# Which token blocks are gathered, and which engine sums the second expert table, in a one-layer decoder step

## The chip, the cores and the metric

The kernel runs on one core of one Trainium2 chip. The metric is the device time of one execution in microseconds; three runs of the kernel before gave 4419.91, 4423.67 and 4437.72, median 4423.67. The profile is of one more execution, of 4433.77 us.

## What is computed

One inference step of a decoder trunk with one layer, on 1024 prompt tokens (blocks 0 to 7 of 128) and 64 sample tokens (8 sequences of 8, "the sample block", numbered 8), with the same weights, D = 1024, all float32.

```
n = rmsnorm(x);  z = n @ w_in
h = x + w_out( sum over 3 branches of sigmoid(gate_b) * P_b(branch_b(n)) )
    branches: gated linear attention (GLA, with a running state),
              forgetting softmax attention (FoX, prompt: causal over earlier blocks;
                                            sample: over a paged cache of 1024 tokens),
              attention over 256 memory tokens
xn = rmsnorm(h)
per token, 8 heads: top 16 of 16384 experts by two sets of 128 keys -> eidx, softmax weights g
a = gelu(xn . u_tab[eidx]);  h += sum over the 128 chosen of (g*a) * v_tab[eidx]
y = rmsnorm(h)
```

Outputs are y, and the new caches and states of prompt and sample.

## The kernel before, in words

**Token groups.** The layer runs over three groups of blocks, `GROUPS = [[0,1,2], [3,4,5], [8,6,7]]` (line 42), one call of `base` (line 636) each, so that a weight tile, loaded once per group, serves up to 384 tokens. `mm_w` (line 256) loads 512 KB of weights (line 262), splits them into a high and a low part on ScalarE and VectorE (lines 265, 267), and TensorE multiplies three products of high and low parts in fp32r (lines 273 to 285). The branches of a block are float32: `gla` (389), `fox_prompt` (550, work grows with the block's number), `mem_prompt_att` (595). The sample block has its own: `gla_sample` (484, its state products at lines 493 and 507), `fox_sample` (1240) and `mem_sample` (1363), which fetch cache pages through GpSimd's queue (line 1237) and sum values in partition strips of one PSUM bank (lines 1348, 1403). `base` ends with h and the normed rows stored (`h_scr`, `x2_scr`), and the key scores, reduced to the best 16 on the way by `top16` (902).

**Experts, two ways.** Gathered blocks (0, 1, 2 beside the layer, 6 and 7 beside the dense pass) are done by `peer_gather` (1028): for each of the 128 choices of a token, GpSimd fetches one row of the first table for all 128 tokens (an indirect DMA of 512 KB, line 1040), VectorE multiplies it with the token's row and sums (1042), ScalarE takes the gelu (1044); then GpSimd fetches the row of the second table (1051) and VectorE adds it, scaled, to `acc` (1057). Four row buffers are used in turn (five in the dense pass). Dense blocks (`DENSE = [3, 4, 5, 8]`, 448 tokens) go through `peer_dense` (1122), which streams both tables through TensorE (lines 1166 to 1216) and multiplies by a weight matrix of tokens and experts. That matrix is made by `expert_weights` (1071) in rounds of 16 tokens: one-hot tiles on VectorE and ScalarE, 16 float32 matmuls (1117) into the PSUM bank `cw`, copies (1118), one store to `c_scr` (1120). For a dense block of the last group (`HERE`, the sample) this is done within `peer_dense`, before its main loop.

**The order.** Each engine's order of instructions is laid down ahead by a planner that plays the program through in time with costs of its own and takes, of the ready instructions, the one with the lowest priority number. `at` (1420) sets that number: the layer has the lowest, `choose` and `expert_weights` follow, gathers come last, block by block (`gather`, 1431):

```
    for grp in GROUPS:
        base(grp)
        ...
        if mine and grp is not GROUPS[-1]:
            gather(mine)
    early.close()
    with ExitStack() as ctx2:
        ...
        peer_dense(ctx2, dn)
```

`early.close()` gives the layer's eight PSUM banks and its work tiles to the dense pass. SP issues all other transfers, in one queue; GpSimd's queue has the indirect ones.

## Time and profile before

| What | Value |
|---|---|
| median of 3 runs | 4423.67 us |
| profiled execution | 4433.77 us |
| its span, first to last instruction | 4432.0 us |
| TensorE busy in the span | 3755.6 us (85%) |
| VectorE busy | 3346.1 us (75%) |
| ScalarE, GpSimd busy | 1796.2 us (41%), 1679.1 us (38%) |
| granted TensorE clock, mean | 0.890 |
| DMA, mean over the span | 258 GB/s |

PE is TensorE's matmul, PEld its weight load, DVE VectorE, ACT ScalarE, POOL GpSimd, SP the engine that issues transfers. Busy time is the union of an engine's instructions; matmul ends are modelled. The granted clock is the share of full speed (2.4 GHz) that TensorE was given; its other level is 1.2 GHz. A float32 matmul appears as two records, an fp32r one as one. Times within the span are counted from its first instruction: group 0 of the layer lies at 0 to 704 us, group 1 at 704 to 1695, group 2 at 1695 to 2960, and then comes the dense pass.

### The profile page before, as it was taken

The numbers are of one execution on the slowest core, as the hardware profiler recorded it, in microseconds if no ns is written. First come the engines' busy times: TensorE is split into PE (matmuls) and PEld (weight loads), VectorE is DVE, ScalarE is ACT, GpSimd is POOL, SyncE is SP. The second block draws the span as 40 slices with busy tenths as digits, with TensorE's granted clock in tenths as the row PEclk, the third lists the DMA queues.
The fourth block names the chain that finished last, engine by engine and source line by source line (L and its number), as shares of the span: only waits on it lengthen the run. The fifth ranks groups of instructions, "written<-read, shape, count | busy, mean of one in ns | idle before, by whom it ended". The sixth has DMA issues, their size and how long they took to land. (4 is left out here: it accounts for less than half of the span.)

```text
span 4432.0 us, 62344 instructions
## 1 busy us (share of the span) xinstructions
PE 3755.6 (85%) x21306; PEld 3288.8 (74%) x21306; DVE 3346.1 (75%) x7924; ACT 1796.2 (41%) x3637; POOL 1679.1 (38%) x1466
## 2 busy tenths in 40 slices
PE   4998998676689775787679979986999999999998
PEld 4886997564378775575556558875999899999997
DVE  3443469988788898888885457578999888888883
ACT  2555444343343333465564334444333223323332
POOL 0000003545644444534455553003445454545530
PEclk8997998787689886677689989997999999999999
DMA  3322457888899987778788899548999999999982
GB/s 110 90 84 70 131 165 227 279 274 294 277 309 332 319 267 242 260 243 273 253 277 287 307 321 320 169 140 289 329 303 339 327 332 337 341 337 327 344 297 81
DMA packets 652340, 1141.32 MB, mean 258 GB/s; under 512 B 62158, under 2 KB 445798, under 8 KB 648439
## 3 DMA queue, kind: packets, MB, share of 16 engines
q0 software_dynamic: 193616, 704.99, 45.6%
q1 hardware_dynamic: 458406, 432.35, 30.3%
q8 instruction: 169, 2.77, 0.2%
q14 instruction: 149, 1.21, 0.1%
HBM read 1073.45 MB, written 63.74 MB: 257 GB/s over the span
## 5 line engine op out<-in xcount | busy, mean ns | idle before, releaser
L1040 POOL DMA_INDIRECT u<-in_peer_u_dram,ei x640 | 783.3, 1224 | 873.2 <-DVE a L1042 347.6
L1051 POOL DMA_INDIRECT v<-in_peer_v_dram,ei x640 | 762.3, 1191 | 865.0 <-DVE acc L1057 452.6
L1042 DVE CUSTOM_DVE_ANT_0 u<-u,x 128x1024 f32<-128x1024 f32 x640 | 774.2, 1219 | 129.9 <-DMA u<-in_peer_u_dram,ei 128.3
L1057 DVE SCALAR_TENSOR_TENSOR acc<-v,a,acc 128x1024 f32<-128x1024 f32 x635 | 811.6, 1278 | 70.6 <-DMA v<-in_peer_v_dram,ei 68.2
L265 ACT ACTIVATE wh<-wr 128x512 fp32r<-128x512 f32 x568 | 354.0, 630 | 595.0 <-PE pj L274 186.2
L267 DVE TENSOR_TENSOR wl<-wr,wh 128x512 fp32r<-128x512 f32 x568 | 386.6, 685 | 219.4 <-PE pj L277 63.8
L1210 PE MATMUL py<-dwh,dvh 128*128 128x448 f32 x1024 | 373.9, 370 | 31.3 <-ACT dwh L1197 28.6
L1187 PE MATMUL pa<-xh,duh 128*128 128x448 f32 x1024 | 384.8, 376 | 1.3 <-ACT duh L1168 1.3
L1188 PE MATMUL pa<-xl,duh 128*128 128x448 f32 x1024 | 379.0, 370 | 0.0
L273 PE MATMUL pj<-aT,wh 128*128 128x384 f32 (+1 forms) x1104 | 367.3, 337 | 11.4 <-ACT X L837 4.5
L1211 PE MATMUL py<-dwl,dvh 128*128 128x448 f32 x1024 | 375.4, 367 | 1.4 <-DVE dwl L1198 1.4
L1212 PE MATMUL py<-dwh,dvl 128*128 128x448 f32 x1024 | 373.4, 368 | 0.3 <-DVE dvl L1206 0.3
L274 PE MATMUL pj<-aT,wh 128*128 128x384 f32 (+1 forms) x1104 | 362.3, 332 | 1.7 <-DVE aT L317 1.7
L281 PE MATMUL pj<-wh,aT 128*128 128x256 f32 x944 | 262.1, 301 | 30.3 <-DVE z L720 10.9
L1205 ACT ACTIVATE dvh<-dvr 128x1024 fp32r<-128x1024 f32 x128 | 134.2, 1059 | 377.2 <-PE py L1211 206.6
L282 PE MATMUL pj<-wh,aT 128*128 128x256 f32 x944 | 258.8, 297 | 2.9 <-DVE aT L847 1.5
L277 PE MATMUL pj<-aT,wl 128*128 128x384 f32 (+1 forms) x1104 | 251.8, 335 | 10.3 <-DVE wl L267 10.1
L1117 PE MATMUL cw<-hot,hot 128*128 128x128 f32 x768 | 173.9, 363 | 92.7 <-ACT stg L1118 73.8
L1190 PE MATMUL pa<-xh,dul 128*128 128x448 f32 x1024 | 240.2, 369 | 0.0
L1117 PEld LDWEIGHTS cw<-hot,hot 128*128 128x128 f32 x768 | 134.8, 248 | 138.1 <-ACT stg L1118 103.3
L1210 PEld LDWEIGHTS py<-dwh,dvh 128*128 128x128 f32 x1024 | 192.4, 189 | 48.6 <-ACT dwh L1197 28.9
L273 PEld LDWEIGHTS pj<-aT,wh 128*128 128x128 f32 x1104 | 213.1, 193 | 17.4 <-ACT X L837 6.6
(475 smaller groups left out, 8439.3 us busy)
## 6 DMA issues: line engine op xcount, KB each, us to landing
wr<-in_w_in_dram SPq DMA_DIRECT2D x168, 512.0 KB, 4.8
dvr<-in_peer_v_dram SPq DMA_DIRECT2D x128, 512.0 KB, 7.5
dur<-in_peer_u_dram SPq DMA_DIRECT2D x128, 512.0 KB, 6.6
dc<-c_scr SPq DMA_DIRECT2D x15, 1792.0 KB, 17.4
wr<-in_w_pq_dram SPq DMA_DIRECT2D x48, 512.0 KB, 4.3
c_scr<-stg SPq DMA_DIRECT2D x24, 1024.0 KB, 6.9
wr<-in_w_out_dram SPq DMA_DIRECT2D x24, 512.0 KB, 4.8
u<-in_peer_u_dram,ei POOLq DMA_INDIRECT x640, 6.2
```

Source lines behind the costliest of these rows:

```text
L267: V.tensor_tensor(wl, raw[:, q2:q2 + 2], wh.bitcast(F32), op=OP.subtract)
L273: PE.matmul(ps, wh[:, i, c], hi[:, k], start=k == 0, stop=False)
L274: PE.matmul(ps, wh[:, i, c], lo[:, k], start=False, stop=False)
L1040: G.indirect_dma_start(out=r, out_offset=None, in_=UR, in_offset=bass.IndirectOffsetOnAxis(ap=ei[:, s:s + 1], axis=0))
L1042: V.tensor_tensor_reduce(r, r, x2, 1.0, 0.0, OP.mult, OP.add, a[:, s:s + 1])
L1051: G.indirect_dma_start(out=r, out_offset=None, in_=VR, in_offset=bass.IndirectOffsetOnAxis(ap=ei[:, s:s + 1], axis=0))
L1057: V.scalar_tensor_tensor(acc, r, a[:, s:s + 1], acc, op0=OP.mult, op1=OP.add)
L1187: PE.matmul(pa[:, :NT], uh[:, k], xh[:, k], start=k == 0, stop=False)
L1188: PE.matmul(pa[:, :NT], uh[:, k], xl[:, k], start=False, stop=False)
L1210: PE.matmul(py[:, :NT], vh[:, j], wh, start=j == 0, stop=False)
L1211: PE.matmul(py[:, :NT], vh[:, j], wl, start=False, stop=False)
L1212: PE.matmul(py[:, :NT], vl[:, j], wh, start=False, stop=j == DG - 1)
```

## The change

The sample block goes into the first group, `GROUPS = [[8,0,1], [2,3,4], [5,6,7]]`. Gathered beside the layer are still 0, 1 and 2 (0 and 1 after group 0, 2 after group 1); beside the dense pass 5 and 6 instead of 6 and 7, by `peer_gather` as before. Dense are 8, 3, 4 and 7; block 7 takes the sample's part as the dense block of the last group.

For 0, 1 and 2, `choose` writes indices and weights in another layout: 64 tokens at a time, partitions 0 to 63 with a token's first four heads and 64 to 127 with its last four. `gather_u` is as before but by halves of a block (64 fetches of 128 rows each). `gather_v` fetches 64 times as well, and TensorE sums: the stationary is a 128x64 matrix with a token's two scales in its column (`st`, eight at a time on VectorE), the moving operand is the fetched row, its first 512 columns going to partitions 0 to 63 of the bank `cw` and its last 512 to 64 to 127. `turns` takes one fetch of the second table's half and one of the next half's first table by turns. `expert_weights` in the layer uses the banks `g` instead of `cw`; the sample's choice and expert weights get the last priority of all; the ring `tp` has two buffers instead of three; `acc` of `peer_gather` lies in the dense pass's pool.

```diff
--- before.py
+++ after.py
@@ -39,13 +39,13 @@
 
 ROWS, ROWS2 = 4, 5
 SAMPLE = 8
-GROUPS = [[0, 1, 2], [3, 4, 5], [SAMPLE, 6, 7]]
-
-DENSE = [3, 4, 5, SAMPLE]
-
-LATER = [6, 7]
-
-HERE = [SAMPLE]
+GROUPS = [[SAMPLE, 0, 1], [2, 3, 4], [5, 6, 7]]
+
+DENSE = [SAMPLE, 3, 4, 7]
+
+LATER = [5, 6]
+
+HERE = [7]
 DG, DW = 8, 9
 WR = 4
 CB = {"hot": 4, "stg": 1, "eg": 1}
@@ -70,8 +70,8 @@
     pp = early.enter_context(tc.tile_pool(name="pp", bufs=8, space=bass.MemoryType.PSUM))
     bp = early.enter_context(tc.tile_pool(name="bp", bufs=1))
 
-    BUFS = {"aT": 2, "wr": WR, "wh": 4, "wl": 2, "z": 4, "zq": 1, "zt": 4, "tq": 2, "tp": 3, "oT": 3, "kv": 2, "pg": 2,
-            "la": 2, "ge": 3, "lh": 4, "kE": 2, "gq": 1, "att": 2, "X": 2, "XL": 2, "P": 4, "PT": 3, "sm": 12,
+    BUFS = {"aT": 2, "wr": WR, "wh": 4, "wl": 2, "z": 4, "zq": 1, "zt": 4, "tq": 2, "tp": 2, "oT": 3, "kv": 2, "pg": 2,
+            "la": 2, "st": 2, "ah": 2, "ge": 3, "lh": 4, "kE": 2, "gq": 1, "att": 2, "X": 2, "XL": 2, "P": 4, "PT": 3, "sm": 12,
             "sm2": 1, "sm5": 1}
     PSB = {"pj": 2, "g": 2, "f": 2, "po": 1, "cw": 1}
     cnt = [0]
@@ -975,7 +975,7 @@
                     V.match_replace(k[:, hd], s[:, hd, 0:8], k[:, hd], 0.0)
                     V.max(s[:, hd, 8:16], k[:, hd])
             c = slice(hf * 64, (hf + 1) * 64)
-            if b in DENSE:
+            if b in DENSE or b not in LATER:
                 ei, gw = w[:, 528:592].bitcast(I32), region(656, 16)
             else:
                 ei, gw = eidx[b][:, c], gate_w[b][:, hs]
@@ -994,19 +994,26 @@
             if b in DENSE:
                 SP.dma_start(e_scr[b][:, c], ei)
                 SP.dma_start(g_scr[b][:, c], w[:, 656:720])
+            elif b not in LATER:
+
+                for i in range(2):
+                    o, x = slice(64 * hf, 64 * hf + 64), slice(64 * i, 64 * i + 64)
+                    V.tensor_copy(eidx[b][o, 64 * i:64 * i + 64], ei[x])
+                    V.tensor_copy(gate_w[b][o, 4 * i:4 * i + 4], gw[x])
 
 
     UR, VR = peer_u[0], peer_v[0]
 
     turn = [0]
     lanes = [gp] * ROWS
+    dense_pool = []
 
     def big(name):
 
         cnt[0] += 1
         turn[0] += 1
         if name in ("x2", "acc"):
-            return gp.tile([128, 1024], F32, tag=name, name=f"{name}_{cnt[0]}", bufs=1)
+            return (gp if name == "x2" else dense_pool[0]).tile([128, 1024], F32, tag=name, name=f"{name}_{cnt[0]}", bufs=1)
         i = turn[0] % len(lanes)
         return lanes[i].tile([128, 1024], F32, tag=f"row{i}", name=f"{name}_{cnt[0]}", bufs=1)
 
@@ -1068,6 +1075,67 @@
         SP.dma_start(gfin, rows(g_final, 1024))
         finish(b, acc, ht, gfin)
 
+
+    halves_of = [(0, 64), (64, 128)]
+
+    def gather_u(b, half, a):
+
+        x2 = big("x2")
+        for lo, hi in halves_of:
+            SP.dma_start(x2[lo:hi], x2_scr[b][64 * half:64 * half + 64])
+        ei, gw = eidx[b], gate_w[b]
+        for hd in range(4):
+            for k in range(16):
+                s = hd * 16 + k
+                r = big("u")
+                G.indirect_dma_start(out=r, out_offset=None, in_=UR,
+                                     in_offset=bass.IndirectOffsetOnAxis(ap=ei[:, 64 * half + s:64 * half + s + 1], axis=0))
+                V.tensor_tensor_reduce(r, r, x2, 1.0, 0.0, OP.mult, OP.add, a[:, s:s + 1])
+                if k == 15:
+                    sl = slice(hd * 16, (hd + 1) * 16)
+                    A.activation(a[:, sl], a[:, sl], AF.Gelu_apprx_tanh)
+                    V.tensor_tensor(a[:, sl], a[:, sl], gw[:, 4 * half + hd, :], op=OP.mult)
+                yield
+
+    def gather_v(b, half, a):
+
+
+        ei = eidx[b]
+        acc = PS("cw")
+
+        PE.matmul(acc, nd[64:65, :128].bitcast(F32), iof[64:65, None, :].to_broadcast([1, 4, 128]), start=True, stop=False)
+        for s in range(64):
+            if s % 8 == 0:
+                st = T("st", [128, 8, 64])
+                V.tensor_tensor(st, id2[:, None, :].to_broadcast([128, 8, 64]),
+                                a[:, s:s + 8, None].to_broadcast([128, 8, 64]), op=OP.mult)
+            r = big("v")
+            G.indirect_dma_start(out=r, out_offset=None, in_=VR,
+                                 in_offset=bass.IndirectOffsetOnAxis(ap=ei[:, 64 * half + s:64 * half + s + 1], axis=0))
+            for i, (lo, hi) in enumerate(halves_of):
+                PE.matmul(acc[lo:hi], st[:, s % 8], r[:, 512 * i:512 * i + 512], start=False, stop=s == 63)
+            yield
+
+        t = big("h")
+        ht, gfin = t[:, :512], t[:, 512:]
+        rs = slice(64 * half, 64 * half + 64)
+        for i, (lo, hi) in enumerate(halves_of):
+            SP.dma_start(ht[lo:hi], h_scr[b][rs, 512 * i:512 * i + 512])
+            SP.dma_start(gfin[lo:hi], bass.AP(tensor=g_final.tensor, offset=g_final.offset + 512 * i,
+                                              ap=[[0, 64], [1, 512]]))
+        V.tensor_tensor(ht, acc, ht, op=OP.add)
+        s1 = gp.tile([128, 2], F32, tag="fs", name=f"fs{b}_{half}", bufs=2)
+        s2 = gp.tile([128, 2], F32, tag="fr", name=f"fr{b}_{half}", bufs=2)
+        A.activation(acc, ht, AF.Square, accum_out=s1[:, 0:1])
+        for i, (lo, hi) in enumerate(halves_of):
+            V.tensor_copy(s2[lo:hi, 0:1], s1[64 - lo:128 - lo, 0:1])
+        V.tensor_tensor(s1[:, 1:2], s1[:, 0:1], s2[:, 0:1], op=OP.add)
+        G.tensor_scalar(s2[:, 1:2], s1[:, 1:2], 1.0 / D, EPS, op0=OP.mult, op1=OP.add)
+        G.tensor_tensor(s2[:, 1:2], s2[:, 1:2], neghalf[:, :1], op=OP.pow)
+        V.scalar_tensor_tensor(ht, ht, s2[:, 1:2], gfin, op0=OP.mult, op1=OP.mult)
+        for i, (lo, hi) in enumerate(halves_of):
+            SP.dma_start(y_prompt[0, b * 128 + 64 * half:b * 128 + 64 * half + 64, 512 * i:512 * i + 512], ht[lo:hi])
+
     def expert_weights(b, H=None, psum=None):
 
         w = 64 if b == SAMPLE else 128
@@ -1078,7 +1146,7 @@
             return bp.tile(shape, dt, tag=tag, name=f"{tag}_{cnt[0]}", bufs=CB[tag])
 
         H = H or H_base
-        psum = psum or (lambda: PS("cw"))
+        psum = psum or (lambda: PS("g"))
 
 
         q, e, f = H("hot", [128, 2, 128]), H("hot", [128, 2, 128]), H("hot", [128, 2, 128])
@@ -1413,6 +1481,8 @@
 
     iof = const([128, 128], F32, cp)
     G.iota(iof, pattern=[[1, 128]], base=0, channel_multiplier=0, allow_small_or_imprecise_dtypes=True)
+    id2 = const([128, 64], F32, cp)
+    V.tensor_tensor(id2, ident[:, :64], ident[:, 64:], op=OP.add)
     mem_kv()
     M = 10 ** 6
     urgent = [M // 2]
@@ -1427,6 +1497,7 @@
 
 
     prio = [M]
+    rest = [100 * M]
 
     def gather(blocks):
         for i, b in enumerate(blocks):
@@ -1435,6 +1506,26 @@
                 at(prio[0] + M // 2, choose, blocks[i + 1])
             at(prio[0], peer_gather, b)
         prio[0] += M
+
+    def gather_halves(blocks):
+
+        v = iter(())
+        for i, b in enumerate(blocks):
+            for half in range(2):
+                prio[0] += M
+                if half and i + 1 < len(blocks):
+                    at(prio[0] + M // 2, choose, blocks[i + 1])
+                a = T("ah", [128, 64])
+                at(prio[0], turns, gather_u(b, half, a), v)
+                v = gather_v(b, half, a)
+        prio[0] += M
+        at(prio[0], turns, v)
+        prio[0] += M
+
+    def turns(*its):
+        its = list(its)
+        while its:
+            its = [x for x in its if next(x, its) is not its]
 
     for grp in GROUPS:
         pj3[0] = grp is GROUPS[0]
@@ -1448,16 +1539,23 @@
         for b in first:
             if b in DENSE and grp is GROUPS[-1]:
                 choose(b)
-            else:
-                at(None, choose, b)
-            if b in DENSE and grp is not GROUPS[-1]:
-                at(None, expert_weights, b)
+                continue
+
+            late = b == SAMPLE
+            if late:
+                rest[0] += M
+            at(rest[0] if late else None, choose, b)
+            if b in DENSE:
+                if late:
+                    rest[0] += M
+                at(rest[0] if late else None, expert_weights, b)
         if mine and grp is not GROUPS[-1]:
-            gather(mine)
+            gather_halves(mine)
     early.close()
     with ExitStack() as ctx2:
         dn = ctx2.enter_context(tc.tile_pool(name="dn", bufs=1))
         lanes += [dn] * (ROWS2 - ROWS)
+        dense_pool.append(dn)
         if mine:
             gather(mine)
         peer_dense(ctx2, dn)
```

## Rows read from the trace of the kernel before

**Rows 1.** Busy us by stage: PE, PEld, DVE, ACT, POOL, (counts); clock, DMA share, GB/s.

```profile
704.00:1695.00 991.00, 747.50 (x4280) 653.75 (x4280) 868.46 (x2276) 383.92 (x779) 490.81 (x433) 0.82 0.87 291
1695.00:2960.00 1265.00, 1005.51 (x5846) 796.18 (x5846) 909.03 (x2377) 614.91 (x1378) 530.40 (x457) 0.83 0.77 261
3064.00:4432.00 1368.00, 1338.27 (x6984) 1227.48 (x6983) 1151.26 (x1900) 419.91 (x669) 614.96 (x501) 0.99 0.88 306
```

**Rows 2.** Three shorter stretches, same columns.

```profile
60.00:704.00 644.00, 594.99 (x3827) 550.44 (x3826) 315.41 (x924) 316.32 (x669) 14.30 (x31) 0.92 0.38 113
1300.00:1400.00 100.00, 91.63 (x505) 86.72 (x504) 90.61 (x182) 43.90 (x71) 49.81 (x41) 1.00 0.94 330
2320.00:2680.00 360.00, 316.06 (x1934) 211.83 (x1933) 194.29 (x357) 143.75 (x321) 196.27 (x175) 0.94 0.87 306
```

**Rows 3.** VectorE's busy us by stage, line 1057 alone, then line 1042 alone.

```profile
704.00:1695.00 991.00, 242.72 (x190) 0.82 0.87 291
1695.00:2960.00 1265.00, 244.02 (x191) 0.83 0.77 261
...
704.00:1695.00 991.00, 255.99 (x419) 0.82 0.87 291
1695.00:2960.00 1265.00, 213.21 (x350) 0.83 0.77 261
```

**Rows 4.** Who waited for whom: us in total, times, longest.

```profile
POOL v L1051 <- DVE acc L1057: 452.6, 250, 10.7
DVE acc L1057 <- DMA v<-in_peer_v_dram,ei: 68.2, 66, 3.5
...
SPq L262 <- DVE wl L267: 781.2, 210, 18.8
```

**Rows 5.** Groups of instructions: busy us, mean ns of one, idle before.

```profile
L267 DVE TENSOR_TENSOR wl<-wr,wh 128x512 fp32r<-128x512 f32 x568 | 386.6, 685 | 219.4 <-PE pj L277 63.8 <-PE pj L285 39.4 <-issue 27.5
...
L1117 PE MATMUL cw<-hot,hot 128*128 128x128 f32 x768 | 173.9, 363 | 92.7 <-ACT stg L1118 73.8 <-DVE hot L1112 12.9 <-DVE a L1042 3.3
...
L1118 ACT ACTIVATE stg<-cw 128x256 f32<-128x256 f32 x192 | 116.8, 608 | 167.7 <-PE cw L1117 125.9 <-DMA c_scr<-stg 41.0
```

**Rows 6.** TensorE's timeline near 2391 us: start, us, instruction.

```profile
2391.09 1.93 PE L1348 MATMUL po<-wr,PT 128*64 128x512 f32 x4
2392.95 0.71 PE L1117 MATMUL cw<-hot,hot 128*128 128x128 f32 x4
```

**Rows 7.** TensorE's timeline near 2672 us.

```profile
2671.90 2.52 PE L1403 MATMUL po<-wr,P 128*32 128x512 f32 x12 [0.47 <-ACT P L99]
2674.99 1.90 PE L1403 MATMUL po<-wr,P 128*32 128x512 f32 x4 [0.57 <-DMA wr<-in_cache_mem_v_dram]
```

**Rows 8.** Line 1117 alone in one stretch: PE, PEld; clock, DMA.

```profile
2320.00:2680.00 360.00, 30.97 (x180) 23.58 (x180) 0.94 0.87 306
```

**Rows 9.** Records of seven lines: duration ns min/median/max, first and last start.

```profile
L1348 PEld LDWEIGHTS po<-wr,PT x128: 132/137/231, 2372.2 to 2585.3; 128*64 128x64 f32 x128
...
L1403 PE MATMUL po<-wr,P x32: 592/594/1062, 2646.4 to 2676.3; 128*32 128x512 f32 x32
...
L493 PE MATMUL g<-X,kv x64: 361/361/380, 1786.6 to 2082.1; 128*128 128x8 f32 x64
...
L507 PE MATMUL g<-XL,kE x16: 1054/1136/1219, 1795.7 to 2106.1; 64*128 64x512 f32 x16
...
L1117 PE MATMUL pc<-dhot,dhot x128: 270/275/582, 2977.0 to 3034.6; 128*128 128x128 f32 x128
...
L907 DVE MAX8 tp<-zt x96: 269/276/296, 634.3 to 1692.3; 128x8 f32<-128x128 f32 x96
...
L1120 SPq DMA_DIRECT2D c_scr<-stg x24: 319/320/424, 1786.7 to 2503.5; - x24
```

**Rows 10.** TensorE's timeline before the dense main loop.

```profile
3063.67 1.11 PE L1210 MATMUL py<-dwh,dvh 128*128 128x448 f32 x2 [28.65 <-ACT dwh L1197]
```

**Rows 11.** DMA issues: KB each, median us to landing.

```profile
t_scr<-tp SPq DMA_DIRECT2D x48, 32.0 KB, 3.1
```

## The prediction

> **What bounds the kernel now.** I read the busy time of each engine by stage first [rows 1]. The cuts are where the first gathers start (704 us), where the second group's last scores are reduced (1695), where the dense pass's own work starts (2960) and where its main loop runs unbroken (3064). In the last stage TensorE is busy for 1338 of 1368 us; the change alters nothing there: two blocks are gathered beside 448 dense tokens before and after. So look at the layer, 0 to 2960. In the stage of group 1 VectorE is busy for 868 of 991 us (88%), TensorE for 748 at a granted clock of 0.82. Between 60 us and 704, with nothing gathered, TensorE is busy for 595 of 644 us at 0.92 and VectorE for half [rows 2]. The gathers take VectorE and leave TensorE with holes, and holes lower its clock. What VectorE gives to them: 243 and 244 us to the sums over the second table in the two stages, 256 and 213 to the products with the first [rows 3]. The waits say the same: GpSimd's gathers wait for VectorE to free a row buffer (452.6 us for second-table rows over the run), seldom the other way round (68.2) [rows 4].
>
> My unit for TensorE is **full-clock work**: busy time times granted clock. Before: 547 (60 to 704), 613 (group 1), 835 (group 2), 1995 us in all [rows 1, 2]. The pace without gathers is 547 of 644, or 0.85; with them 0.62 and 0.66.
>
> **The change part by part.** The sum is made against the profiled execution, 4433.8 us (span 4432.0), which is 10.1 above the median of the runs.
>
> *VectorE's sums go.* Three layer blocks have 384 of them, 190 + 191 recorded, 487 us [rows 3]. In their place come 48 builds of the scaled stationary, 512 elements each, by the nearest VectorE row of that size 0.685 us [rows 5]: 33 us. The copies of indices and weights are 24 far smaller ones, under 16 us by the same row, 4 taken; the finish of a block has the same elements in six half-width pieces instead of three, nothing on balance, hidden in VectorE's new room. The net is -450 of 1777 us.
>
> *TensorE's sums come.* Each gathered row tile needs two float32 matmuls of 128x64 by 512 columns, into partitions 0 to 63 and 64 to 127 of one bank. A float32 matmul shows as two records. On one column strip, two such matmuls (four records) take 1.86 us to the next start, or 1.93 with the tail [rows 6]. Four strips of 32 show the other end: one strip's four records take 1.90 us, yet twelve records, three strips, take 2.52 [rows 7]; strips run side by side. For two strips of 64 the floor is half of four records in a row, at 2.52/12 = 0.21 us each 0.84; the ceiling is 1.93. On one strip records start (1.90 - 0.592)/3 = 0.436 apart [rows 7, 9], so I take 1.0: two rounds of 0.43 and some 0.15 for going in and out of the form (1.86 less four of them, 0.12 to 0.14). 384 x 1.0 = 384 us (323 to 741). The Trainium skill, TensorEngine Tiling, Key Properties, says that changing the tiling mode, not just the tile, drains the engine. The trace agrees so far as the 0.15 goes; without a drain the sum would be 58 us of work lower.
>
> *The sample block moves into group 0.* Its cache attentions are nearly all of the stretch 2320 to 2680: 316 us busy at 0.94 is 297, less 31 x 0.94 of expert weights, 268 [rows 2, 8]. Its state part is 64 x 0.361 + 16 x 1.136 = some 40 [rows 9]. Group 0 loses 128 prompt tokens and gains 64: between a sixth and a third of 547, 91 to 182; 110 taken, near the low end since projections go by columns. So group 0 has 547 - 110 + 308 = 745, at 0.85 it ends at 60 + 876 = 936, and gathers start 230 us later. The GpSimd fetches of the sample's cache move too, out of the gathers' queue. Total work of the three groups stays.
>
> *What is left.* 1995 - 745 = 1250 of work, less some 25 (the layer prepares expert weights of 320 tokens instead of 384, a sixth of the 174 us busy in [rows 5], at 0.83), plus 384: 1609. VectorE would need 1777 - 450 = 1327 in the same time, so TensorE is what fills up. What pace? The sums wait for nothing of the layer and fill its holes, so at least 0.85, the pace with nothing to fill; above that, the queue is in order, and a late row holds layer work. I take 0.86: 1871 us, end at 2807, **153 earlier**. At 0.80 it is 2947 (13 earlier), at 0.92 it is 2685 (275).
>
> *Block 7 in the expert pass.* It takes the sample's place in the last group: the choice covers 128 partitions either way, so that it costs the same, but its expert weights are 128 tokens instead of 64. Those are made between the layer and the dense pass, where TensorE then waits: four rounds of 16 tokens run from 2977.0 to 3034.6, and the first second-table matmul starts at 3063.67 after 28.65 us idle [rows 9, 10]. Four rounds more cost 57.6 us at that pace; 35 if only their matmul records counted, one after the other (128 x 0.275); more than 57.6 isn't excluded, as block 5's choice is on VectorE then. I take **+55**.
>
> *Small ones.* A ring of two instead of three for top-16 results: its store lands in 3.1 us [rows 11], while VectorE's next result takes about 2.8 (ten passes of 0.276 [rows 9]); 48 results at under 1 us, 0 to 48, mostly beside other work: **+10**. Expert weights take the transposes' banks ("g", two) instead of the bank that the sums now own. 20 rounds of 8 hold one bank for a matmul group and a ScalarE copy of 0.608 us [rows 5]: 160 x about 1.3 = 208 us of two banks' time, 0 to 60 of delay: **+15**. SP issues 48 transfers for x2, h, the gain and the result instead of 12, 0.32 us each [rows 9]: 12 us more, and its waits for x2's single buffer and for a free row buffer come six times instead of three. Queued behind them are weight loads. Nothing taken: SP waits for VectorE to free weight buffers for 781 us anyway, and four are loaded ahead; if that cover fails, 12 such waits at SP's mean of 3.7 us (781.2/210 [rows 4]) cost 45. POOL issues as many gathers as before; ScalarE, the same.
>
> Sum: 4433.8 - 153 + 55 + 10 + 15 = 4361; less the 10 to the median, rounded: **4350 us**, 1.7% faster.
>
> **The rivals.**
>
> *Transfers bound the layer* (slower). The two gather stages moved 291 x 0.991 + 261 x 1.265 = 618 MB [rows 1]; some 42 of it (64 page fetches and 16 memory loads of 512 KB) go into group 0. 576 MB in 1871 us is 308 GB/s. Against: 330 in a good stretch [rows 2], 306 over the dense stage. For: group 1 averaged only 291 at a share of 0.87 [rows 1], with transfers already waited on. At 291 the layer takes 1979 us and ends at 2915, 45 earlier, and the 80 us of extras make it 4459. It decides from where the rate falls under 296 GB/s (576 MB in the 1944 us that just pay for the extras), with the gathers still running when the layer ends: the dense pass can't have its PSUM before the last sum is out. Chance 0.13.
>
> *Late rows hold TensorE's queue* (slower). VectorE waited 68.2 us in 66 waits for second-table rows [rows 4], 1.03 each. On TensorE such a wait stops projections. Each costs 1.03, so 71 of 384 rows eat the 73 us of net gain; if half wait it is 198 us: 4549. For: order is fixed by planned times, and transfers are at 0.87. Against: rows are fetched four buffers ahead, and only a tenth waited. Chance 0.08.
>
> *The strips don't run side by side* (slower). At 1.93 each 741 us: (1225 + 741)/0.86 = 2286, end at 3222, 4766. Against it stand [rows 7], of strips half as wide. The Trainium skill, TensorE: Matmul & The Clock Gate, Part 3, lets weight loads overlap running matmuls only where the row group differs, and both strips use all rows. By that rule, as a mechanism here: four loads of 0.137 us [rows 9] stand open, 384 x 0.55 = 210 us more, 4595; the trace speaks against it, since twelve records in 2.52 us leave no room for open loads. Chance 0.04 for both.
>
> *Gain and price cancel* (same). At a pace of 0.82 the layer takes 1962 us and ends 62 earlier, against extras of 80: 4442; at 0.83, 4419. Chance 0.13. It is also where the sums' leaving VectorE does nothing, because the layer was held by its own chains: group 0's 0.85 with VectorE half idle speaks against that.
>
> **How the numbers follow.** Forecast: 0.62, its own range 4230 to 4400. About 0.5%, 22 us, is what a measurement of this kernel tells from no change: faster under 4401, slower over 4446. Faster 0.63 (the forecast and a little of the transfers' case at a better rate), same 0.13, slower 0.24. Low end: pace 0.92 gives 4228. High end: the transfers' case and half of the late rows': 4490. Below and above are some 0.08 and 0.12.
>
> **What would show it.** VectorE under 75% after the first group, TensorE's clock there over 0.9, first gathers near 940, sums over v at about a microsecond of TensorE, the dense stage starting near 2860 to 2870 after a gap some 55 us longer. Wrong: gathers that end after the layer's last scores; TensorE's waits for v over 100 us; records of the two halves one after the other; a dense main loop of another length than 1368 us.

## The result and the profile after

The kernel after takes 4914.97 us (median; 4906.32 to 4918.60), the kernel before beside it 4430.69 (4419.91 to 4437.78): ratio 1.1092, 95% interval 1.1060 to 1.1125. It is slower by some 484 us, where 4350 us was forecast, and far outside the range. The profiled execution has a span of 4916.1 us.

The page's 40 slices, 122.9 us each, show where to look. TensorE's busy share and its granted clock, in tenths:

```profile
PE   5979989606998998757578989997599999999998
...
PEclk8888999757997999858569999998699999999999
```

The ninth digit, 983 to 1106 us, is a 0; once TensorE had started, its longest idle time before was the 28.65 us of [rows 10]. The 18th and 20th, within 2090 to 2460, are 5, with the clock at 0.5 both times. The stages of the kernel after, cut where its scores and main loop fall, answer to [rows 1, 2] (columns as there: window, its length, busy us and count of TensorE, weight loads, VectorE, ScalarE, GpSimd; granted clock; DMA share, GB/s):

```profile
60.00:990.00 930.00, 808.95 (x5272) 671.83 (x5271) 360.58 (x1231) 351.45 (x753) 82.73 (x105) 0.89 0.42 127
990.00:2078.00 1088.00, 852.39 (x4582) 611.45 (x4582) 676.24 (x1921) 389.13 (x810) 462.66 (x435) 0.86 0.79 265
2078.00:3360.00 1282.00, 1048.44 (x5487) 723.81 (x5487) 642.92 (x2025) 517.87 (x1152) 395.32 (x387) 0.85 0.66 216
965.00:1101.00 136.00, 1.59 (x6) 0.63 (x5) 113.96 (x487) 9.14 (x20) 68.22 (x60) 0.50 0.69 230
2078.00:2498.00 420.00, 255.53 (x904) 123.55 (x903) 246.40 (x979) 159.25 (x412) 188.29 (x172) 0.65 0.76 254
3360.00:3534.00 174.00, 106.13 (x508) 91.27 (x507) 151.54 (x584) 98.80 (x237) 58.39 (x49) 0.67 0.78 273
3534.00:4916.00 1382.00, 1344.51 (x6984) 1234.62 (x6984) 1115.81 (x1766) 420.99 (x666) 561.42 (x475) 0.98 0.85 293
```

VectorE is freed as meant, 62% and 50% busy beside the gathers, and neither it nor the transfers (0.79, 0.66) nor TensorE is full. The full-clock work of groups 1 and 2 is 852 x 0.86 + 1048 x 0.85 = 1624 us, forecast 1609; but it takes 2370 us instead of 1871. The pace (full-clock work per us) is 0.69. So the work came out near the sum, and the time went into holes.

The two largest holes are cut out in the fourth and fifth lines. Group 0's last scores are multiplied at 965 us. Then TensorE's timeline reads (start, length, engine, line, tiles; in brackets the idle time before and what ended it):

```profile
964.20 1.22 PE L890 MATMUL f<-c,tq 128*128 128x128 f32 x4 [3.64 <-ACT zt L99]
1093.80 0.69 PE L1161 MATMUL g<-c,hot 128*128 128x128 f32 x2 [128.38 <-DVE hot L1158]
...
1100.99 2.10 PE L1185 MATMUL g<-hot,hot 128*128 128x128 f32 x8 [1.85 <-DVE ch L948]
```

After 128 us of nothing come the sample's expert weights (lines 1161 and 1185), and only behind their four rounds, at 1187 us, the first small projection of group 1's layer (line 682): 222 us after the scores. In the kernel before it stood 7 us after them (717), 13 in the next group. At the next border the hole is 422 us. Its end:

```profile
2496.34 2.05 PE L1185 MATMUL g<-hot,hot 128*128 128x128 f32 x8 [1.25 <-ACT stg L1186]
2498.24 1.92 PE L314 MATMUL g<-c,wr 128*128 128x128 f32 x8
2500.04 0.28 PE L682 MATMUL f<-P,aT 128*128 128x24 f32 x1
```

Line 314 is the first thing that a group's layer does on TensorE: it transposes the normed rows, into a bank of `g`. It starts with the last expert round of blocks 3 and 4 and needs nothing of theirs but the bank. That the sample's rounds had the last priority of all did not help; the layer waited for them nevertheless.

The waits for the new sums (in total, times, longest) and the groups of instructions (busy us, mean ns, idle before) answer to [rows 3 to 5]:

```profile
POOL v L1113 <- PE cw L1116: 579.7, 231, 19.6
PE cw L1116 <- DMA v<-in_peer_v_dram,ei: 167.9, 100, 6.7
PE g L1161 <- DVE hot L1158: 128.4, 1, 128.4
```

```profile
L1116 PE MATMUL cw<-v,st 128*64 128x512 f32 x1536 | 498.6, 707 | 169.0 <-DMA v<-in_peer_v_dram,ei 167.9 <-DVE tp L911 0.7
L1110 DVE TENSOR_TENSOR st<-c,ah 128x512 f32<-128x512 f32 x48 | 32.8, 686 | 34.7 <-PE cw L1116 34.2
```

GpSimd waits longer for a free row buffer than before, for TensorE now: 579.7 us against 452.6 [rows 4]. All records of the sums are in the trace, 498.6 / 384 = 1.30 us a row, at the stages' clock 1.1 us of full-clock work.

### The profile page after: what moved, and what is told of

Same layout as the page of the kernel before. It is cut to its first block, busy times and chain, and to the rows that moved or that the text cites. A ratio compares the mean times of both kernels' runs of the same rounds, so it can differ in the third digit from the quotient of the medians.

```text
span 4916.1 us, 65107 instructions
## 1 busy us (share of the span) xinstructions
PE 4167.4 (85%) x22854; PEld 3338.6 (68%) x22854; DVE 2968.3 (60%) x7637; ACT 1786.6 (36%) x3631; POOL 1565.7 (32%) x1472
## 5 line engine op out<-in xcount | busy, mean ns | idle before, releaser
L1116 PE MATMUL cw<-v,st 128*64 128x512 f32 x1536 | 498.6, 707 | 169.0 <-DMA v<-in_peer_v_dram,ei 167.9
L1091 POOL DMA_INDIRECT u<-in_peer_u_dram,ei x384 | 430.4, 1121 | 602.4 <-DVE ah L1093 388.5
L1113 POOL DMA_INDIRECT v<-in_peer_v_dram,ei x384 | 402.1, 1047 | 672.2 <-PE cw L1116 579.7
L1047 POOL DMA_INDIRECT u<-in_peer_u_dram,ei x256 | 314.7, 1229 | 471.4 <-DVE a L1049 175.6
L1058 POOL DMA_INDIRECT v<-in_peer_v_dram,ei x256 | 299.0, 1168 | 366.4 <-DVE acc L1064 208.9
L273 PE MATMUL pj<-aT,wh 128*128 128x384 f32 (+1 forms) x1104 | 373.3, 341 | 5.9 <-ACT kv L99 3.0
L274 PE MATMUL pj<-aT,wh 128*128 128x384 f32 (+1 forms) x1104 | 367.9, 335 | 0.1
L1116 PEld LDWEIGHTS cw<-v,st 128*64 128x64 f32 x1536 | 97.1, 150 | 345.7 <-DMA v<-in_peer_v_dram,ei 242.0
L1064 DVE SCALAR_TENSOR_TENSOR acc<-v,a,acc 128x1024 f32<-128x1024 f32 x254 | 324.5, 1278 | 7.1 <-DMA v<-in_peer_v_dram,ei 5.7
L1273 ACT ACTIVATE dvh<-dvr 128x1024 fp32r<-128x1024 f32 x128 | 134.1, 1057 | 358.9 <-PE py L1279 237.2
L281 PE MATMUL pj<-wh,aT 128*128 128x256 f32 x944 | 253.3, 292 | 10.1 <-DVE z L863 3.6
L282 PE MATMUL pj<-wh,aT 128*128 128x256 f32 x944 | 250.9, 288 | 0.0
```

The source lines that it names most:

```text
L273: PE.matmul(ps, wh[:, i, c], hi[:, k], start=k == 0, stop=False)
L274: PE.matmul(ps, wh[:, i, c], lo[:, k], start=False, stop=False)
L1091: G.indirect_dma_start(out=r, out_offset=None, in_=UR, in_offset=bass.IndirectOffsetOnAxis(ap=ei[:, 64 * half + s:64 * half + s + 1], axis=0))
L1113: G.indirect_dma_start(out=r, out_offset=None, in_=VR, in_offset=bass.IndirectOffsetOnAxis(ap=ei[:, 64 * half + s:64 * half + s + 1], axis=0))
L1116: PE.matmul(acc[lo:hi], st[:, s % 8], r[:, 512 * i:512 * i + 512], start=False, stop=s == 63)
```

## The experiments

Every kernel's places in the trace, in us: the last scores of the three groups; the wait from a group's last scores to line 682 of the next; when block 2's gather is finished (its result is squared for the norm); the first matmul of the dense pass's main loop. The ratios have before in the same session under them, with 95% intervals.

| kernel | last scores | waits | block 2 | main loop | median | ratio |
|---|---|---|---|---|---|---|
| before | 710, 1669, 2941 | 7, 13 | 2764 | 3064 | 4430.69 | 1 |
| after | 965, 2078, 3352 | 222, 422 | 3123 | 3534 | 4914.97 | 1.109 (1.106 to 1.113) |
| e1 | 712, 1663, 3208 | 7, 529 | 2569 | 3339 | 4702.66 | 1.063 (1.059 to 1.066) |
| e2 | 964, 1891, 2840 | 3, 3 | 3334 | 3482 | 4848.06 | 1.095 (1.092 to 1.098) |
| e3 | 963, 1915, 2915 | 10, 10 | 2955 | 3101 | 4475.36 | 1.011 (1.007 to 1.016) |
| e4 | 957, 2055, 3277 | 246, 459 | 2784 | 3455 | 4838.02 | 1.092 (1.089 to 1.095) |
| e5 | 967, 1863, 2766 | 4, 3 | 3029 | 3414 | 4780.76 | 1.079 (1.077 to 1.082) |
| e6 | 964, 1884, 2833 | 10, 10 | 2838 | 3283 | 4642.14 | 1.048 (1.046 to 1.051) |
| e7 | 964, 2010, 3179 | 3, 3 | 3038 | 3360 | 4731.29 | 1.069 (1.066 to 1.070) |
| e8 | 975, 2014, 3202 | 3, 2 | 3061 | 3374 | 4743.63 | 1.072 (1.069 to 1.075) |
| e9 | 966, 1871, 2741 | 4, 2 | 3123 | 3175 | 4539.90 | 1.023 (1.020 to 1.026) |
| e10 | 967, 1891, 2820 | 3, 0 | 3316 | 3167 | 4581.44 | 1.034 (1.030 to 1.037) |
| e11 | 716, 1610, 2836 | 3, 2 | 3056 | 3049 | 4399.58 | 0.992 (0.989 to 0.995) |
| e12 | 718, 1726, 2986 | 3, 6 | 2994 | 3111 | 4490.54 | 1.016 (1.013 to 1.019) |

The theory that the profile after suggested, called A: the banks of a PSUM ring are handed out in the order in which the program's text asks for them, whatever the priorities; `expert_weights` stands in the text ahead of the next group's `base`, so that group's transposes wait for all its rounds.

**e1: the kernel before, with its expert weights on `g`.**

```diff
-        psum = psum or (lambda: PS("cw"))
+        psum = psum or (lambda: PS("g"))
```

> The kernel before with one edit: the layer's expert weights take their PSUM from the transposes' two banks (g) instead of their own bank (cw). Theory A, the ring: banks of a ring are handed out in the order of the program text, in which the expert weights of group 1 stand ahead of the layer of group 2, so that group 2's first transposes (line 314) and small projections (line 682) must wait for the last expert matmul (line 1117). Expected: line 682 of group 2, 13 us after group 1's last scores in the kernel before, comes only after all 24 rounds, 300 to 450 us later; the run takes 4650 to 4850 us. Theory B, TensorE's own load (sums and late rows): no sums on TensorE here, so 4425 to 4450 us, the 15 us of the forecast at most.

Measured: 6.3% slower from this line alone. Group 2's layer stands still until the 24 rounds of 3, 4 and 5 (1743 to 2181) are through:

```profile
2179.42 2.05 PE L1117 MATMUL g<-hot,hot 128*128 128x128 f32 x8 [1.15 <-ACT stg L1118]
2181.33 1.97 PE L314 MATMUL g<-c,wr 128*128 128x128 f32 x8
...
2191.96 0.37 PE L682 MATMUL f<-P,aT 128*128 128x24 f32 x1
```

The wait at that border goes from 13 to 529 us. In the kernel before the same rounds ran from 1766 to 2502, beside the layer, and nobody waited. Group 1 is not touched (1663 against 1669): no dense block is chosen ahead of it.

**e2: the kernel after, with its expert weights back on `cw`** (the same line the other way round).

> The changed kernel with that one edit undone: expert weights take the bank cw, which they now share, one buffer, with the sums' accumulator. Theory A: group 1's line 682 starts within 30 us of group 0's last scores (222 us in the changed kernel), group 2's too (422 us), and most of 590 us comes back, less what the wait of sums and expert weights for one bank costs: 4350 to 4600 us. Theory B: the sums still load TensorE and late rows still stop its queue: 4850 to 4950 us. Theory C, the move of the sample block: it stays, so nothing but a part comes back: 4800 to 4900.

Measured: the holes at the borders are gone, 3 us each, and the layer's last scores come at 2840, 512 us earlier than in the kernel after. Yet the time falls by 67 us only, since the main loop starts at 3482: now the sums and the experts share one bank in text order. The rounds of 3 and 4 wait for the sums of 0 and 1 (until 2547), run until 2996, and block 2's sums wait for them. From then until 3334 the engines do little else. TensorE and GpSimd in that stretch, then the stretch as a whole:

```profile
3099.51 0.94 POOL L1113 DMA_INDIRECT v<-in_peer_v_dram,ei  x1 [1.72 <-PE cw L1116]
3101.20 1.97 PE L1116 MATMUL cw<-v,st 128*64 128x512 f32 x4 [1.97 <-DMA v<-in_peer_v_dram,ei]
```

```profile
3000.00:3320.00 320.00, 193.85 (x486) 32.98 (x484) 34.28 (x193) 1.24 (x4) 118.47 (x124) 0.64 0.64 199
```

TensorE waits for the row, GpSimd for the buffer: 320 us for 121 rows (486 records / 4), 2.6 us each. The dense pass can't begin, since the bank is one of the eight that it takes over. So A is right about the banks, and something stands behind it. (The time is where theory C, that the move costs, had it; e3 rules C out.)

**e3: the move alone,** before with the new groups, sums on VectorE, experts on `cw`.

```diff
-GROUPS = [[0, 1, 2], [3, 4, 5], [SAMPLE, 6, 7]]
+GROUPS = [[SAMPLE, 0, 1], [2, 3, 4], [5, 6, 7]]
-DENSE = [3, 4, 5, SAMPLE]
+DENSE = [SAMPLE, 3, 4, 7]
```

(`LATER` and `HERE` as in the change.)

> The kernel before with the new token groups alone: sample in group 0, block 7 in the expert pass, VectorE still sums, expert weights in their own bank. Theories A and B: no loss but the four more rounds of block 7's expert weights ahead of the dense pass (55 to 60 us) and later gathers (they start near 960 instead of 714): 4440 to 4560 us. Theory C, the move is what costs: 4750 us or more.

Measured: 40 us slower. The layer ends 26 us earlier, the entry to the dense pass (last scores to main loop) takes 186 us instead of 123, 63 more.

**e4: the move, and the expert weights on `g`.**

> The run before this one (groups moved, VectorE sums) with the expert weights in the transposes' banks. Theory A: the layer of group 1 waits for the sample's 4 rounds (100 to 200 us) and that of group 2 for 16 (200 to 400 us): 300 to 450 us over the run without that edit, 4750 to 5000. Theory B: the same as without that edit, within 20 us.

Measured: 363 us more than e3 (8.1% of before), with VectorE summing. The two stretches of waiting:

```profile
957.00:1116.00 159.00, 0.51 (x3) 0.29 (x2) 131.83 (x499) 11.42 (x16) 87.02 (x76) 0.50 0.78 252
2055.00:2514.00 459.00, 149.88 (x528) 119.81 (x527) 379.93 (x1102) 161.58 (x416) 237.80 (x198) 0.50 0.81 266
```

TensorE has next to nothing in the first and a third in the second, at the lower level of its clock throughout. With e1 this settles A: without the sums on TensorE the layer waits as long at the borders (246 and 459 us against 222 and 422).

**e5 and e6: all 28 expert rounds at the entry to the dense pass,** with TensorE's sums (e5, from after) and VectorE's (e6, from e3). The call in the groups is taken out of both:

```diff
         for b in DENSE:
-            if b in GROUPS[-1]:
+            if True:
                 expert_weights(b, DT, lambda: DP("c"))
...
-                for x in (slice(0, ready), slice(ready, NS)) if g == 0 else (slice(0, NS),):
+                for x in (slice(0, NS),):
```

> The changed kernel, but all expert weights (28 rounds) are made at the entry of the dense pass, so none stands in the layer. What is left beside the layer is the gathers with TensorE's sums. Theory A (no hold by expert weights, the forecast's pace holds): groups 1 and 2 start within 30 us of the scores before them, and the layer's last scores come at 2760 to 2850. Theory B (TensorE's own load and late rows): they come at 3000 or later. Theory D (the gathers themselves are slow with TensorE's sums, two row buffers for each table): whatever the layer does, the last row of block 2 is summed 100 us or more after the last scores, and the dense pass waits for its PSUM. To be compared with the next run.

> The same with VectorE's sums: the moved groups (run e3), all expert weights at the entry of the dense pass. 20 rounds at 14 to 16 us on e3's time less some relief of the layer: 4700 to 4800 us, last scores at 2850 to 2900. Theory A: e5's last scores are 50 to 120 us earlier than here. Theory B: e5's are later. Theory D: here the dense pass doesn't wait for gathers, in e5 it does, so that e5's whole time is no better or worse.

Measured: with no rounds in the layer TensorE's sums end it at 2766, VectorE's at 2833: 67 us for the change's idea. But e5 is 139 us slower than e6 (4642, less than the 4700 to 4800 that were expected). Its stages, the layer's two and the two of the entry, and e6's:

```profile
990.00:1863.00 873.00, 741.90 (x4151) 551.75 (x4151) 595.70 (x1810) 343.93 (x693) 373.07 (x357) 0.91 0.84 277
1863.00:2766.00 903.00, 827.47 (x4657) 603.90 (x4655) 549.69 (x1698) 364.84 (x750) 354.20 (x342) 0.94 0.78 257
2766.00:3030.00 264.00, 142.28 (x393) 27.24 (x391) 116.75 (x642) 8.41 (x15) 126.07 (x128) 0.71 0.80 264
3030.00:3414.00 384.00, 236.44 (x1156) 197.75 (x1156) 346.55 (x879) 274.67 (x728) 177.61 (x150) 0.71 0.91 319
```

```profile
990.00:1884.00 894.00, 667.74 (x3859) 583.94 (x3858) 777.60 (x1970) 354.91 (x717) 453.99 (x387) 0.83 0.87 291
1884.00:2833.00 949.00, 701.50 (x3807) 593.55 (x3807) 806.60 (x1910) 366.78 (x737) 491.27 (x420) 0.80 0.86 288
2833.00:3283.00 450.00, 269.01 (x1157) 226.03 (x1156) 410.41 (x1464) 294.18 (x742) 169.52 (x144) 0.60 0.79 268
```

In the layer VectorE falls from 85% to 61% in group 2 and the clock rises from 0.80 to 0.94. Then, 2766 to 3030, 264 us pass in which TensorE has little but block 2's sums: 97 rows at 2.7 us. The DMA issues of 2900 to 3019 (count, median us from issue to landing):

```profile
v<-in_peer_v_dram,ei POOLq DMA_INDIRECT x60, 5.5
```

A row lands 5.5 us after its issue, and its buffer comes free only when TensorE has summed it. This is theory D: gathers whose rows TensorE sums, at the lowest priority, end after the layer, and the bank of their sums holds the dense pass.

**e7: the rounds of the kernel after on `g`, but written between the next group's projections.** `expert_weights` is made a generator (`yield` after each store to `c_scr`), is put on a list instead of being run, and one round is taken after each weight tile:

```diff
+            one_round()
...
-                at(rest[0] if late else None, expert_weights, b)
+                todo.append(expert_weights(b))
```

> The changed kernel with its expert weights still in the transposes' banks, but written round by round between the projections of the next group's layer, so that a ring position of the layer stands behind one round at most. Theory A: line 682 follows the last scores within 30 us in groups 1 and 2; last scores at 2800 to 2900; 4350 to 4500 us. Theory B: 4800 or more, as the sums still load TensorE. Theory D: the last scores come early, but sums of block 2 run on for 100 to 300 us, 4500 to 4650.

Measured: with the same ring, the same rounds and no new resource the borders' waits fall from 222 and 422 to 3 us, for another place in the text (the rounds of 3 and 4 had the layer's priority already; the sample's get it here). That is A's mechanism shown from the other side. The time falls by 184 us only, less than expected. The layer stays slow:

```profile
967.00:2010.00 1043.00, 843.85 (x4606) 608.79 (x4605) 686.30 (x2081) 393.93 (x816) 453.70 (x428) 0.88 0.82 273
2010.00:3179.00 1169.00, 999.74 (x5346) 691.83 (x5347) 632.15 (x1953) 509.72 (x1139) 407.75 (x395) 0.91 0.72 238
```

The pace is (844 x 0.88 + 1000 x 0.91) / 2212 = 0.75, against 0.82 in e5. Part of it is in TensorE's own waits over groups 1 and 2: 155.5 us for late rows (83.3 in e5) and 98 for tiles of the rounds that VectorE and ScalarE had not made yet, 53.1 of them in one wait. Which of the many other users of the two banks waits for a round was not tried.

**e8: e7, with block 1's last sums alternating with block 2's first products** instead of running alone between them.

> The run before this one, and the second-table fetches of block 1's last half alternate with the first-table fetches of block 2 instead of running alone. Theory D: the last sum comes 50 to 150 us earlier than in e7, and the whole time falls by as much, if it was the gathers that held the dense pass. Theory A: within 20 us of e7.

Measured: 12 us more than e7, within the 20 us of theory A; block 2 ends at 3061 instead of 3038. The order of the fetches at that border was not what makes the gathers late.

**e9: e5, with block 2 summed on VectorE** (TensorE sums 0 and 1; `choose` writes the new layout for 0 and 1 alone, and `acc` lies in the pool that outlives the layer).

```diff
-            gather_halves(mine)
+            (gather if 2 in mine else gather_halves)(mine)
```

> As the kernel with all 28 rounds at the entry of the dense pass and TensorE's sums (median 4780.76; last scores 2766, block 2's last sums 3019, rounds 3050 to 3391, main loop from 3414), with one difference: block 2 is gathered and summed whole on VectorE, into SBUF, and TensorE sums blocks 0 and 1 alone. Theory that the dense pass waits for the PSUM bank in which block 2 is summed: nothing of block 2 holds the entry now, the rounds start within 100 us of the layer's last scores (near 2790 to 2840), the main loop starts at 3180 to 3260, and the time is 4550 to 4630. Rival, that the rounds or VectorE's own work hold the entry and the bank is only seen beside it: the main loop stays after 3340 and the time above 4700.

Measured: 241 us faster than e5, a little under the expected span. The rounds start at 2775 and the main loop at 3175, although block 2's own gather ends at 3123, later than in e5: it now runs beside the entry.

```profile
1871.00:2741.00 870.00, 785.62 (x4528) 594.23 (x4526) 570.80 (x1651) 361.71 (x745) 367.34 (x340) 0.95 0.80 265
2741.00:3175.00 434.00, 258.24 (x1159) 216.90 (x1158) 402.19 (x1313) 287.76 (x738) 163.50 (x148) 0.64 0.84 287
```

D is shown: not the late gather costs, but the bank that it holds. And against e6 the sums of two blocks on TensorE now *gain* 102 us.

**e10: e2, with block 2 summed on VectorE.** Beside e9's edits to the gathers, the scales of 16 rows share the buffer of `acc`.

> The kernel after with the expert weights on the bank cw again, as in the run that gave 4848.06, and block 2 summed whole on VectorE into SBUF (scales of 16 rows at a time in one buffer instead of eight in two). In that run block 2's sums stood behind the experts of 3 and 4 in cw until 2996, and the entry behind the sums until 3334. Theory of the held bank: that whole stretch goes, the experts of 3 and 4 end by 2900, the main loop starts at 3020 to 3130, and the time is 4400 to 4490, about that of the kernel before. Rival (gathers simply late): the main loop after 3250, the time over 4600.

Measured: 267 us faster than e2, but 91 above the top of what was expected. The stretch of lone sums is gone; the rounds of 3 and 4, though, start in `cw` at 2587 only, when block 1's last sums are out (2582), and take until 3003. The entry is held by the rounds instead. And here the gathers end the kernel: the last block's result is normed at 4565, after the dense blocks' (4545).

**e11: the kernel before, with blocks 0 and 1 summed on TensorE.** Groups and order of before, experts on `cw`; in the text all sums of 0 and 1 stand ahead of all rounds. The call is shown against the kernel before; for the rest, the run has the gathers of e10 and the change's ring `tp` of two buffers.

```diff
-            gather(mine)
+            gather_halves(mine[:2])
+            at(prio[0], choose, 2)
+            gather(mine[2:])
```

> The kernel before with its own groups and order (sample block last, expert weights on cw), in which TensorE sums blocks 0 and 1 and VectorE block 2. The sums have cw from about 704 until 2100 to 2300, the experts of 3, 4 and 5 follow in it during the last group, nothing holds the layer's banks or the entry. If TensorE's sums are worth what the runs with all rounds at the entry showed (67 us over three blocks) and are not paid back at the entry: the layer's last scores at 2860 to 2920 against 2941, the time 4360 to 4420, a gain of up to 1.6%. Rival, that gathers with TensorE's sums run late whatever follows them: experts of 3 to 5 after 2450, the main loop after 3100, the time 4450 to 4600.

Measured: faster than before, 0.9917 (0.9887 to 0.9947), some 34 us and as expected; the layer ends still earlier than that. The stages of the layer in [rows 1], 704 to 1695 and 1695 to 2960:

```profile
704.00:1695.00 991.00, 865.35 (x4910) 658.91 (x4911) 679.97 (x2172) 401.72 (x815) 412.68 (x385) 0.91 0.80 266
1695.00:2960.00 1265.00, 1065.17 (x6243) 775.66 (x6241) 804.89 (x2292) 585.04 (x1337) 513.24 (x488) 0.87 0.81 272
```

VectorE falls from 868 to 680 us, the clock rises from 0.82 to 0.91, and the last scores come 59 and 105 us earlier. 90 of the 105 are lost at the entry (213 us against 123): the rounds of 3 to 5 get `cw` at 2190 and end at 2932.

**e12: e11, with block 0 alone on TensorE** (`mine[:1]`, `mine[1:]`).

> The kernel of the run that gave 4399.58 (ratio 0.9917), in which TensorE sums block 0 alone and VectorE blocks 1 and 2. There the sums had cw until 2190 and the experts of 3, 4 and 5 ended at 2932, 96 us after the layer's last scores (2836): the entry to the dense pass took 213 us where the kernel before has 123. If the bank's hand-over sets the entry, it is free here near 1450, the experts end before 2500, the entry is back to some 125 us; VectorE has a third of the sums' relief instead of two thirds, so the last scores come at 2860 to 2900: main loop at 2985 to 3025, time 4340 to 4390. Rival, that VectorE's relief is what counts and the hand-over is hidden anyway: last scores at 2890 to 2930, main loop from 3040 to 3060, time 4400 to 4430.

Measured: 1.6% slower than before; neither time was hit. The entry is 125 us, as the hand-over of the bank would have it. The layer, however, ends at 2986, 45 us after the kernel before:

```profile
704.00:1695.00 991.00, 833.99 (x4576) 629.81 (x4577) 613.19 (x1915) 368.99 (x756) 369.43 (x349) 0.89 0.75 244
1695.00:2300.00 605.00, 424.46 (x2226) 338.45 (x2225) 524.93 (x1543) 315.61 (x736) 299.51 (x244) 0.70 0.80 263
```

The rounds run from 1820 to 2556, about where the kernel before has them (1766 to 2502), beside VectorE's work for blocks 1 and 2: VectorE is at 87% there and TensorE at 0.70 of its clock, much as in the kernel before (85% and 0.72 from 1766 to 2300). The 45 us are not lost there. Group 1's last scores already come 57 us later than before (1726 against 1669), and from there group 2 takes 1260 us against 1272. Why group 1 is slower, with VectorE down from 868 to 613 us and TensorE up from 748 to 834 in the first line's stage, is open.

## Why the prediction was wrong, step by step

**Group 0** was to end at 936; its scores come at 965, and at 963 with VectorE's sums. Its work was 809 x 0.90 = 728 us, forecast 745; its pace to the last scores 0.80, not 0.85:

```profile
60.00:965.00 905.00, 808.53 (x5272) 671.71 (x5271) 337.56 (x1058) 349.77 (x749) 81.71 (x104) 0.90 0.43 130
```

**The price of TensorE's sums**, 1.0 us a row, holds: with the tail, a row's four records take 1.97 us at the clock's lower level (the row of e2 above; granted 0.50 there) and 1.08 at its upper one (1.00), in e5's timeline:

```profile
2944.24 1.08 PE L1116 MATMUL cw<-v,st 128*64 128x512 f32 x4 [1.04 <-DMA v<-in_peer_v_dram,ei]
```

The sums alone in e5's group 2 (busy us of matmuls and weight loads, clock, DMA):

```profile
1863.00:2766.00 903.00, 185.70 (x636) 38.84 (x636) 0.94 0.78 257
```

That is 159 rows at 1.10 us of full-clock work each. The strips run side by side; the rival in which they don't is out. The Trainium skill, TensorE: Matmul & The Clock Gate, Part 3, says that a weight load overlaps running matmuls only where the row group differs, and both strips use all rows. The measurement decides against that here: two rounds of 0.43 us leave 0.2 of the 1.08, and four loads of 0.137 us one after the other would take 0.55.

**VectorE's relief** is right: 62% and 50%, under the 75% that was asked for. TensorE's clock there, 0.86 and 0.85, stayed under the 0.9 of the forecast; in e5 and e9, without the holes, it is 0.91 to 0.95.

**The pace** of 0.86 for groups 1 and 2 failed in the kernel after (0.69). Outside the two holes it is (851 x 0.90 + 793 x 0.95) / 1839 = 0.83:

```profile
1101.00:2078.00 977.00, 851.22 (x4579) 610.93 (x4579) 585.31 (x1608) 381.67 (x794) 395.45 (x377) 0.90 0.79 264
2498.00:3360.00 862.00, 792.91 (x4585) 600.26 (x4585) 396.52 (x1047) 358.62 (x741) 207.03 (x216) 0.95 0.61 198
```

So 0.86 was too high by a little, and e5's layer, where no round stands in the way, runs at 0.82. It has 675 + 778 = 1453 us of work; with some 120 for the rounds that it leaves for later (20 of 24, 145 us busy by [rows 5], at 0.83) 1573, where 1609 was summed. The unit takes a window's mean clock and so depends on the cuts: with the holes cut out the kernel after has some 1685 us of work instead of 1624, and its agreement with 1609 is in part luck. The rival of late rows has a share: TensorE waited 167.9 us in 100 waits, over the 100 us named as a sign, 68.4 of them within the second hole; in e5's layer, without the holes, it is 83.3 in 52.

**Block 7 in the expert pass**, +55, holds: the entry takes 182 us instead of 123, +59; in e3, +63.

**The main loop** takes 1382 us against 1368, a sign of being wrong that had been named; where these 14 us come from is not shown.

**The step that failed** is the second of the small ones: "Expert weights take the transposes' banks", at 0 to 60, taken at +15. It measured 267 us in the kernel before (e1) and 363 in the moved one (e4 against e3). It counted for how long a bank is held, 160 times 1.3 us, and took the delay for a part of that. That is the wrong question: a ring has an order, and the layer's first tile comes after the last round's. So the layer waits from a group's last scores to the end of the last round, choice and all, with TensorE largely idle: 529 us in e1, 246 and 459 in e4. About half of these waits is seen in the whole time; that rounds and gathers done meanwhile no longer burden the layer would explain it, but is not shown. The diff showed the tag, the text showed the order, and the last priority given to the sample's rounds should have warned: work with the last priority stood ahead of work with the first in a queue that knows none.

**A second term** was missing: what holds the dense pass's banks when the layer is done. It was named within the rival of the transfers ("the dense pass can't have its PSUM before the last sum is out") and tied to a rate under 296 GB/s, as the price of full transfers. e5 shows it at 264 us, with 257 to 277 GB/s in the layer but a share of 0.78 to 0.84, where 0.94 was reached before [rows 2]: the transfers were not full, and the lone sums go at the pace of a row's round trip through its buffers. In the kernel after itself it doesn't decide, because the layer is later still (scores at 3352, block 2 out at 3123).

The account: 4436 before; +40 for the move (e3); +363 for the bank (e4); +77 for TensorE's sums on top of both, with the smaller ring `tp` and the sample's last priority, which were not tried alone: 4915. The order matters. From e3, the sums with the experts on `cw` (and the same two small edits) cost 373 (e2), and the bank on top only 67. That each alone breaks the overlap of rounds, layer and sums, and the second finds little left to break, would fit these runs, but is argued.

## What to carry to other kernels

Before a tile is moved to another ring, read the ring in the order of the text: in these runs whoever asked next waited for everyone who had asked before, whatever the priorities said, and a background task that stands ahead of the main line in such a ring is the main line. Count a shared bank by who is behind it, not by how long it is held. And a resource that the next phase takes over (here PSUM) must not be in the hands of the slowest filler: the same sums that cost 139 us when the last block was among them gained 102 when it was not.

## What was not expected of the hardware

When the sums of one block ran alone (e2), TensorE was busy for 194 of 320 us at a granted clock of 0.64, the transfers' share was 0.64, and each row took 2.6 us instead of 1.1. Neither was full: TensorE waited for rows, and GpSimd for TensorE to free one of the four row buffers; a row took 5.5 us from issue to landing in e5. And two strips of 64 columns, each with all 128 rows and its own weights, finished four records in 1.08 us at granted clock 1.00 (e5), where one strip's four take 1.86 [rows 6].
